# The transposed stream is made again for each use, and its 16 KB per partition become a tenth weight tile

## The chip, the cores and the metric

One core of one Trainium2 chip. The metric is the device time of one execution in microseconds (us); the kernel before takes 1452.84 us (median of 3 runs, 1452.74 to 1452.98).

## The reference

One layer on 256 tokens of width 2048, all in fp32: a mixer (attention and a state-space scan behind shared projections), then `h = layer_norm(alpha * x + mix)`, and on that h

```
scores = sigmoid(h @ w_router);  two experts of 16 per token, from one group of four
moe    = sum_e combine[:, e] * ((silu(h @ w_gate[e]) * (h @ w_up[e])) @ w_down[e])
ple    = sigmoid(h @ w_ple_gate) * (p @ w_ple)          # w_ple_gate is 2048 x 2048
out    = layer_norm(alpha * h + moe + ple)
```

The weights of one expert are 24 MB and those of the per-layer gate (with `w_ple`) 18 MB, so some 400 MB are read for this second half.

## The kernel before, in words

`front` (to line 531) computes the mixer. `back` (from line 534) is the second half, and the change lies there.

**Weight tiles.** Every weight of the second half passes through tiles of 128x4096 fp32 (2 MB of 2^20 bytes, 16 KB per partition) that the class `Ring` (line 42) hands out. `plan_loads` (line 74) lists the loads in the order in which they are used: for each expert e four pairs of gate and up tiles ("g" and "u", 2 MB each) and four down tiles ("d"); behind an expert of `PLE_AT` the three parts of one chunk of the per-layer gate ("pg": 1, 2 and 1 MB, with 0.5 MB of `w_ple`). `take` gives a tile to the matmuls and puts its room behind the spare ones; `fill` issues the next loads into what is spare, on SP's queue, where each waits until the last matmul that read its room is done. The rooms go round, so with N of them a load waits for the use N tiles earlier. There are 2 tiles in `ring1`, 2 in `ring2`, 4 in `ring3` (line 540), and one that is used once (`bonus`, line 586): nine at the start, eight from expert 1 on. SP's queue issues loads and little else.

**The h and its transposed copy.** `h` (tokens on partitions, 16 KB per partition, normalised but without gain and bias) stays to the end. `hT` (line 567) is the same, transposed, with gain and bias: 16 blocks k of 128x256, made once in lines 593 to 606 by TensorE transposes of h into a PSUM tile with two blocks, whose even block VectorE and whose odd block ScalarE then writes to `hT`. Besides the router, three things read it: `ple_gate` (line 825), `residual` (line 906) and the body of `overflow` (line 847), which runs only if an expert got over 64 tokens. At the end `ln2` lies in its room (line 568): gain and bias of the last norm, written behind expert 13.

**The order of the work.** `phase()` (line 675) ties TensorE's instructions of a phase behind the last one of the phase before; inside a phase a scheduler orders them, at compile time. For each expert: `gate_up` (line 716; 128 matmuls of 128x64 by 512 columns, which run side by side in pairs), `hidden` (line 729) with the other half of the expert before (`return_half`, line 799), for experts 2, 4, 5 and 7 a chunk of `residual`, at expert 7 `overflow` with its branch, behind odd experts `gather` (line 694) of the tokens for the next two, then `down` (line 781), and behind experts 3, 7, 10 and 12 a chunk of `ple_gate`: for 16 blocks k and two halves t of the tokens a matmul of 128x128 by 512 columns, then 8 matmuls with `w_ple`. Behind `down` ScalarE and VectorE split its result (`split_y`, line 776).

**Small tiles.** The pool `mp` (line 538) has tags with one room each: "xg" and "y" (8 KB), "w2" (2 KB; `hid` and `sg` use it), "hidT" (2 KB). PSUM tags "mt" and "pl" have two banks each.

Of the kernel before, what the change touches and what calls it, by code (L numbers as in the profile page):

```python
# [7 lines left out]
F32 = mybir.dt.float32  # L8
# [17 lines left out]
R = 4  # L26
PLE_AT = (3, 7, 10, 12)
RES_AT = (2, 4, 5, 7)
# [13 lines left out]
class Ring:  # L42


    def __init__(self):
        self.loads, self.n, self.pools, self.spare, self.tiles = [], 0, [], [], {}
        self.once = None

# [18 lines left out]
    def take(self, key):  # L67
        t, j = self.tiles.pop(key)
        if j != self.once:
            self.spare.append(j)  # L70
        return t
# [462 lines left out]
def back(ctx, tc, i, out, fr, dbg=lambda *a: None):  # L534
# [4 lines left out]
    psum = ctx.enter_context(tc.tile_pool(name="psum2", bufs=1, space=PSUM))  # L539
    ring.add(ctx.enter_context(tc.tile_pool(name="ring3", bufs=1)), RING3)  # L540
    ring.fill()

# [23 lines left out]

    hT = mp.tile([128, KB, 256], F32, name="hT")
    ln2 = hT.rearrange("p (j k) t -> p j (k t)", j=2)
    stats(5)
# [23 lines left out]
    for k2 in range(8):  # L593
        ps = banks[k2].rearrange("p (k t) -> p k t", k=2)
        for r in range(2):
            k = 2 * k2 + r
            for t in range(NT):
                nc.tensor.transpose(ps[:, r, t * 128:(t + 1) * 128], h[:, t, k * 128:(k + 1) * 128], ident)
        for r in range(2):
            k = 2 * k2 + r  # L600
            if r:
                nc.scalar.activation(hT[:, k, :], ps[:, r, :], AF.Identity, bias=lnT[:, 1, k:k + 1],
                                     scale=lnT[:, 0, k:k + 1])
            else:
                nc.vector.tensor_scalar(hT[:, k, :], ps[:, r, :], lnT[:, 0, k:k + 1], lnT[:, 1, k:k + 1],
                                        op0=OP.mult, op1=OP.add)
# [5 lines left out]
    for k in range(KB):  # L612
        g = k % 4
        nc.tensor.matmul(pr4[32 * g:32 * g + 32], fr.wr[:, k, :], hT[:, k, :], start=k < 4, stop=k >= KB - 4)
    r4 = mp.tile([128, 256], F32, name="r4", tag="cm", bufs=2)
# [113 lines left out]
    def hidden(e, pgu, oh, between):  # L729
# [15 lines left out]
        for j in range(4):  # L745
            nc.tensor.transpose(ps[:, j, :], hid[:, j // 2 * 256 + j % 2:(j // 2 + 1) * 256:2], ident)  # L746
        hidT = mp.tile([128, 4, 128], F32, name="hidT")
        nc.scalar.activation(hidT, ps, AF.Copy)
# [56 lines left out]
    def down_last(e, hidT, cm):  # L805
        py = psum.tile([128, 2, 512], F32, name="py", tag="y", bufs=1)
        y = y_parts()
        for q in range(4):
# [11 lines left out]
            for t in range(NT):  # L820
                for dh in range(2):
                    c = 4 * dh + q
                    nc.vector.bn_stats(st[:, t, c, :], acc[:, t, c * 256:(c + 1) * 256])

    def ple_gate(c):
        cs = slice(c * 512, (c + 1) * 512)
        pg = [pl_psum() for _ in range(NT)]
        for g, (k0, k1) in enumerate(PLE_PARTS):
            w = v2(ring.take(("pg", c, g)), 512)
            for k in range(k0, k1):  # L830
                for t in range(NT):
                    nc.tensor.matmul(pg[t], hT[:, k, t * 128:(t + 1) * 128], w[:, k - k0, :],  # L832
                                     start=k == 0, stop=k == KB - 1)
            if k1 < KB:
                ring.fill()
# [11 lines left out]
    def overflow():  # L847
# [9 lines left out]
        with tc.If(n_over > 0):  # L857
            with tc.For_i(0, NE, 1) as e:
# [3 lines left out]
                hd = mp.tile([128, 512], F32, name="hd", tag="w2", bufs=1)  # L862
                ow2 = mp.tile([128, 2, 512], F32, name="ow", tag="y")
                ow = ow2[:, 0, :], ow2[:, 1, :]
                for fh in range(2):
                    pgs = [psum.tile([128, 512], F32, name="pgu", tag="gu", bufs=2) for _ in range(NT)]
                    pus = [pl_psum() for _ in range(NT)]
                    for k in range(KB):
                        for j, (src, pz) in enumerate(((i["w_gate"], pgs), (i["w_up"], pus))):
                            w = wload(ow[j], src, e, k // R * 128 * R + k % R, fh * 512, R)  # L870
                            for t in range(NT):
                                nc.tensor.matmul(pz[t], hT[:, k, t * 128:(t + 1) * 128], w,
                                                 start=k == 0, stop=k == KB - 1)
# [32 lines left out]
    def residual(c):  # L906

        for t in range(NT):
            ps = pl_psum()
            for r in range(R):  # L910
                nc.tensor.transpose(ps[:, r * 128:(r + 1) * 128], hT[:, R * c + r, t * 128:(t + 1) * 128], ident)
            a = acc[:, t, c * 512:(c + 1) * 512].rearrange("p (f r) -> p r f", r=R)
            nc.vector.scalar_tensor_tensor(a, ps.rearrange("p (r f) -> p r f", r=R), ALPHA, a, op0=OP.mult, op1=OP.add)

    last = None
    for e in range(NE):
        if e % 2 and e + 1 < NE:
            oh_next = onehot(e + 1)
        with phase():
            pgu = gate_up(e, xg)  # L920
# [3 lines left out]
        hidT, cm = hidden(e, pgu, oh, lambda c: last and return_half(*last, c))  # L924
        if e in RES_AT:
            with phase():
                residual(RES_AT.index(e))
        if e == OV_AT:
# [16 lines left out]
        if e == 0:  # L945
# [15 lines left out]
            nc.vector.tensor_copy(ovT, po)  # L961
            nc.gpsimd.dma_start(scro, ovT)
        if e in PLE_AT:
            with phase():
                ple_gate(PLE_AT.index(e))
        if e == LN2_AT:

            for j in range(2):
                for c in range(4):
# [47 lines left out]
```

## Time and profile before

| | us |
|---|---|
| median of 3 runs | 1452.84 |
| the profiled execution | 1453.28 |
| its span | 1451.2 |
| TensorE matmul busy in the span | 1358.4 (94%) |
| VectorE busy | 453.5 (31%) |
| ScalarE busy | 296.9 (20%) |
| GpSimd busy | 62.1 (4%) |
| moved by DMA, mean rate | 499.91 MB, 344 GB/s |
| mean granted TensorE clock | 0.984 |

The span is that of one execution; the 2.1 us between span and time of that execution lie outside of it. Matmuls are pipelined, so that the busy time of one overlaps the next: what TensorE takes for a stretch is read from start to start. A timeline row gives the start, the busy time, engine and line, and in brackets how long the engine had been idle before and what it waited for.

### The profile page before, as it was taken

The page shows a single profiled execution, that of the slowest core. Times are in us where ns is not written, and L with a number is a line of the kernel's source. Part 1 is how long each engine was busy: PE and PEld are TensorE (multiplying, and loading weights), DVE is VectorE, ACT ScalarE, POOL GpSimd, SP SyncE. Part 2 cuts the span into 40 slices and gives each one's busy share as a digit, 9 for nine tenths or more (in the row PEclk, how much of TensorE's full clock was granted, in tenths as well). Part 3 has the DMA queues.
Part 4 walks back from the last instruction along what each step waited for, and adds up shares of the span by engine and source line. Part 5 has one row for each costly group of instructions (what it writes and reads, how often), then busy time and mean ns, then how long its engine had stood idle before and what let it go on. Part 6 is the DMA issues. An engine that isn't in the chain of part 4 may idle for free. (4 is left out here: it accounts for less than half of the span.)

```text
span 1451.2 us, 15673 instructions
## 1 busy us (share of the span) xinstructions
PE 1358.4 (94%) x6595; PEld 735.2 (51%) x6595; DVE 453.5 (31%) x768; ACT 296.9 (20%) x477; POOL 62.1 (4%) x80
## 2 busy tenths in 40 slices
PE   7999999999988999889999886999989999999994
PEld 5877888787785343344334323433423343445332
DVE  4486784646553020220023112002211031020227
ACT  4475564545332010000001000100100010002000
POOL 3000011301000000000000000000000000000002
PEclk9999999999998999999999999999999999999997
DMA  8655446456937999999999999999999999999994
GB/s 276 200 166 184 160 147 201 147 188 226 357 126 321 427 426 427 427 427 413 428 425 427 427 427 420 359 406 426 427 427 413 427 428 421 419 425 426 427 393 159
DMA packets 89646, 499.91 MB, mean 344 GB/s; under 512 B 9684, under 2 KB 22396, under 8 KB 65252
## 3 DMA queue, kind: packets, MB, share of 16 engines
q1 hardware_dynamic: 88128, 495.41, 84.8%
q0 software_dynamic: 1408, 3.41, 0.8%
q8 instruction: 53, 0.87, 0.2%
q14 instruction: 21, 0.17, 0.0%
q10 hardware_dynamic: 36, 0.05, 0.0%
HBM read 496.68 MB, written 2.16 MB: 344 GB/s over the span
## 5 line engine op out<-in xcount | busy, mean ns | idle before, releaser
L724 PE MATMUL pgu<-ring,xg 128*64 128x512 f32 x2048 | 450.2, 595 | 33.1 <-DMA ring<-in_w_up 18.2
L724 PEld LDWEIGHTS pgu<-ring,xg 128*64 128x64 f32 x2048 | 145.7, 137 | 334.4 <-issue 289.1
L790 PE MATMUL py<-ring,hidT 128*64 128x512 f32 x960 | 210.8, 594 | 7.4 <-DMA ring<-in_w_down 6.4
L207 DVE TENSOR_TENSOR wl<-ring,wh 128x1024 fp32r<-128x1024 f32 x128 | 156.2, 1224 | 140.0 <-ACT wh L206 134.8
L206 ACT ACTIVATE wh<-ring 128x1024 fp32r<-128x1024 f32 x128 | 135.4, 1060 | 172.1 <-PE pj L213 144.7
L211 PE MATMUL pj<-wh,xh 128*128 128x512 f32 x384 | 153.8, 402 | 1.1 <-ACT xh L188 1.0
L212 PE MATMUL pj<-wl,xh 128*128 128x512 f32 x384 | 153.6, 400 | 0.0
L213 PE MATMUL pj<-wh,xl 128*128 128x512 f32 x384 | 152.6, 399 | 0.0
L790 PEld LDWEIGHTS py<-ring,hidT 128*64 128x64 f32 x960 | 67.0, 137 | 141.3 <-issue 124.4
L734 DVE TENSOR_TENSOR hid<-hid,pgu 128x512 f32<-128x512 f32 x16 | 11.0, 688 | 399.7 <-ACT hid L733 399.7
L832 PE MATMUL pl<-ring,hT 128*128 128x512 f32 x256 | 110.9, 594 | 0.0
L779 DVE TENSOR_TENSOR y<-py,y 128x512 fp32r<-128x512 f32 (+1 forms) x34 | 22.5, 660 | 223.8 <-ACT y L778 223.8
L733 ACT ACTIVATE hid<-pgu 128x512 f32<-128x512 f32 x16 | 9.6, 598 | 390.9 <-PE pgu L724 390.9
L768 DVE SCALAR_TENSOR_TENSOR acc<-bk,cw,acc 128x512 f32<-128x512 f32 (+1 forms) x128 | 81.7, 710 | 1.9 <-PE bk L763 1.9
L211 PEld LDWEIGHTS pj<-wh,xh 128*128 128x128 f32 x384 | 72.6, 189 | 18.3 <-ACT xh L188 2.1
L213 PEld LDWEIGHTS pj<-wh,xl 128*128 128x128 f32 x384 | 72.4, 189 | 16.6 <-DVE xl L189 0.2
L212 PEld LDWEIGHTS pj<-wl,xh 128*128 128x128 f32 x384 | 72.6, 189 | 16.1
L832 PEld LDWEIGHTS pl<-ring,hT 128*128 128x128 f32 x256 | 48.3, 190 | 62.6 <-issue 62.6
L703 PE MATMUL mt<-wr,h 128*128 128x128 f32 x512 | 64.0, 289 | 7.9 <-PEq L857 6.1
L778 ACT ACTIVATE y<-py 128x512 fp32r<-128x512 f32 (+1 forms) x34 | 19.5, 573 | 238.6 <-PE py L790 209.7
L703 PEld LDWEIGHTS mt<-wr,h 128*128 128x128 f32 x512 | 62.5, 204 | 10.3 <-PEq L857 6.3
L212 PE MATMUL pj<-wl,moh 128*128 128x512 f32 (+1 forms) x160 | 56.7, 354 | 0.5 <-DVE wl L207 0.5
(252 smaller groups left out, 934.8 us busy)
## 6 DMA issues: line engine op xcount, KB each, us to landing
ring<-in_w_gate SPq DMA_DIRECT2D x64, 2048.0 KB, 22.9
ring<-in_w_up SPq DMA_DIRECT2D x64, 2048.0 KB, 24.5
ring<-in_w_down SPq DMA_DIRECT2D x60, 2048.0 KB, 25.8
ring<-in_w_in SPq DMA_DIRECT2D x48, 1024.0 KB, 5.1
ring<-in_w_out SPq DMA_DIRECT2D x16, 1024.0 KB, 6.5
ring<-in_w_ple_gate SPq DMA_DIRECT2D x16, 1024.0 KB, 30.8
ring<-in_w_down SPq DMA_DIRECT2D x32, 256.0 KB, 6.0
xq<-in_x SPq DMA_DIRECT2D x8, 256.0 KB, 9.4
```

The lines of the kernel that those rows point to most:

```text
L206: nc.scalar.activation(h, v, AF.Copy)
L207: nc.vector.tensor_tensor(l, v, h.bitcast(F32), op=OP.subtract)
L211: nc.tensor.matmul(ps, ah, bh, start=first, stop=False)
L212: nc.tensor.matmul(ps, ah, bl, start=False, stop=False)
L213: nc.tensor.matmul(ps, al, bh, start=False, stop=last)
L703: nc.tensor.matmul(ps[:, k % 4], h[:, t, cols], oh[:, t], start=t == 0, stop=t == 1)
L724: nc.tensor.matmul(pgu[j][hs], xg[:, k, e % 2, :], w[:, r, fh * 512:(fh + 1) * 512], start=k == 0, stop=k == KB - 1)
L768: nc.vector.scalar_tensor_tensor(a, ps[dh], cw[:, t, e:e + 1], a, op0=OP.mult, op1=OP.add)
L778: nc.scalar.activation(yh, ps, AF.Copy)
L779: nc.vector.tensor_tensor(yl, ps, yh.bitcast(F32), op=OP.subtract)
L790: nc.tensor.matmul(py[hs, c, :], hidT[:, j, fh * 64:(fh + 1) * 64], w[:, r, dh * 1024 + c * 512:dh * 1024 + (c + 1) * 512], start=fb == 0, ...
L832: nc.tensor.matmul(pg[t], hT[:, k, t * 128:(t + 1) * 128], w[:, k - k0, :], start=k == 0, stop=k == KB - 1)
```

## The change

`hT` is no longer kept. For the router it is still made once, in two halves that lie in the rooms of "xg" and "y". Afterwards `turn` transposes two blocks of h at a time into an "mt" bank and writes them with gain and bias into a small tile `hb`, whose rooms are those of "w2" and "hidT" in turn; `ple_gate` calls it before each even k, `residual` twice per chunk. In `turn` the order is: two transposes of the even block, its write by VectorE, two transposes of the odd block, its write by ScalarE. The 16 KB become `ring4`, one tile more; from expert 13 on, that tile is not given out again and holds `ln2`. The second chunk of the gate comes behind expert 8 rather than 7, and its loads with it. `residual` moves from before `down` to behind it (so behind overflow and gather too), since "hidT" is in use until `down` is done. The `overflow` body makes its blocks anew as well.

```diff
-PLE_AT = (3, 7, 10, 12)
+PLE_AT = (3, 8, 10, 12)
...
-        self.once = None
+        self.once = self.retire = None
...
-        if j != self.once:
+        if j not in (self.once, self.retire):
             self.spare.append(j)
...
     ring.add(ctx.enter_context(tc.tile_pool(name="ring3", bufs=1)), RING3)
+    ring.add(ctx.enter_context(tc.tile_pool(name="ring4", bufs=1)), 1)
+    last_pool = len(ring.pools) - 1
     ring.fill()
...
-    hT = mp.tile([128, KB, 256], F32, name="hT")
-    ln2 = hT.rearrange("p (j k) t -> p j (k t)", j=2)
+    hT = []
+    for tag in ("xg", "y"):
+        part = mp.tile([128, 8, 256], F32, name="hT", tag=tag)
+        hT += [part[:, k, :] for k in range(8)]
...
+    def turn(dst, k2, n=2):
+        ps = mt_psum([128, n, 256])
+        for r in range(n):
+            k = n * k2 + r
+            for t in range(NT):
+                nc.tensor.transpose(ps[:, r, t * 128:(t + 1) * 128], h[:, t, k * 128:(k + 1) * 128], ident)
+            if r:
+                nc.scalar.activation(dst[:, r, :], ps[:, r, :], AF.Identity, bias=lnT[:, 1, k:k + 1],
+                                     scale=lnT[:, 0, k:k + 1])
+            else:
+                nc.vector.tensor_scalar(dst[:, r, :], ps[:, r, :], lnT[:, 0, k:k + 1], lnT[:, 1, k:k + 1],
+                                        op0=OP.mult, op1=OP.add)
+        return dst
+
+    def turned(k2):
+        return turn(mp.tile([128, 2, 256], F32, name="hb", tag=("w2", "hidT")[k2 % 2], bufs=1), k2)
...
             for k in range(k0, k1):
+                if k % 2 == 0:
+                    hb = turned(k // 2)
                 for t in range(NT):
-                    nc.tensor.matmul(pg[t], hT[:, k, t * 128:(t + 1) * 128], w[:, k - k0, :],
+                    nc.tensor.matmul(pg[t], hb[:, k % 2, t * 128:(t + 1) * 128], w[:, k - k0, :],
                                      start=k == 0, stop=k == KB - 1)
...
-        for t in range(NT):
-            ps = pl_psum()
-            for r in range(R):
-                nc.tensor.transpose(ps[:, r * 128:(r + 1) * 128], hT[:, R * c + r, t * 128:(t + 1) * 128], ident)
+        pss = [pl_psum() for _ in range(NT)]
+        for k2 in (2 * c, 2 * c + 1):
+            hb = turned(k2)
+            for t, ps in enumerate(pss):
+                for r in range(2):
+                    col = (2 * (k2 % 2) + r) * 128
+                    nc.tensor.transpose(ps[:, col:col + 128], hb[:, r, t * 128:(t + 1) * 128], ident)
+        for t, ps in enumerate(pss):
...
+        if e == LN2_AT:
+            ring.retire = last_pool
...
-        if e in RES_AT:
-            with phase():
-                residual(RES_AT.index(e))
         if e == OV_AT:
             overflow()
...
+        if e in RES_AT:
+            with phase():
+                residual(RES_AT.index(e))
         if e in PLE_AT:
...
+            ln2 = v2(ring.tile(last_pool), DM)
```

## Rows read from the trace of the kernel before

**Rows 1.** The page, its second part: the span in 40 slices of 36.3 us, busy share of the DMA engines in tenths and GB/s moved.
```profile
DMA  8655446456937999999999999999999999999994
GB/s 276 200 166 184 160 147 201 147 188 226 357 126 321 427 426 427 427 427 413 428 425 427 427 427 420 359 406 426 427 427 413 427 428 421 419 425 426 427 393 159
```

**Rows 2.** Timeline of TensorE in the gate and up matmuls of expert 3: the first and the last of eight tiles.
```profile
603.63 3.65 PE L724 MATMUL pgu<-ring,xg 128*64 128x512 f32 x16 [1.34 <-DMA ring<-in_w_gate]
...
637.87 3.65 PE L724 MATMUL pgu<-ring,xg 128*64 128x512 f32 x16 [1.26 <-DMA ring<-in_w_up]
```

**Rows 3.** Busy time in stretches of 10 us. Columns: stretch, its length, then busy us and instructions of TensorE (PE), weight load (PEld), VectorE (DVE), ScalarE (ACT) and GpSimd (POOL); granted TensorE clock, DMA share, GB/s.
```profile
450.00:460.00 10.00, 10.00 (x70) 8.76 (x70) 3.01 (x6) 3.02 (x8) 0.00 (x0) 0.85 0.45 190
460.00:470.00 10.00, 10.00 (x50) 3.41 (x48) 0.00 (x0) 0.00 (x0) 0.00 (x0) 1.00 0.70 269
...
920.00:930.00 10.00, 10.00 (x38) 3.70 (x35) 1.38 (x2) 1.20 (x2) 0.00 (x0) 1.00 0.60 220
...
950.00:960.00 10.00, 10.00 (x33) 3.82 (x33) 1.38 (x2) 1.20 (x2) 2.53 (x2) 1.00 0.88 342
```

**Rows 4.** Timeline of SP's queue before the first expert: the first of four tiles of `ring3`, then `bonus` and the three behind it.
```profile
428.22 0.34 SPq L83 DMA_DIRECT2D ring<-in_w_gate  x1
...
434.42 34.72 SPq L83 DMA_DIRECT2D ring<-in_w_down  x4
```

**Rows 5.** Timeline of TensorE from the last up tile of expert 7 to the first of expert 8.
```profile
886.93 3.65 PE L724 MATMUL pgu<-ring,xg 128*64 128x512 f32 x16 [1.26 <-DMA ring<-in_w_up]
...
901.21 10.13 PE L703 MATMUL mt<-wr,h 128*128 128x128 f32 x64 [6.10 <-PEq L857]
911.27 13.95 PE L790 MATMUL py<-ring,hidT 128*64 128x512 f32 x64
925.15 27.73 PE L832 MATMUL pl<-ring,hT 128*128 128x512 f32 x64
...
956.25 27.69 PE L724 MATMUL pgu<-ring,xg 128*64 128x512 f32 x128
```

**Rows 6.** The instructions of line 857 (the branch of `overflow`) on SP's queue: duration in ns, first and last start in us.
```profile
L857 SPq EVENT_SEMAPHORE  x8: 17/17/17, 916.6 to 924.8; - x8
```

**Rows 7.** Timeline of TensorE: the gate and up matmuls of experts 9 and 10 begin, the third chunk of the per-layer gate, expert 11 begins.
```profile
1001.20 27.64 PE L724 MATMUL pgu<-ring,xg 128*64 128x512 f32 x128
...
1053.40 13.90 PE L724 MATMUL pgu<-ring,xg 128*64 128x512 f32 x64
...
1106.37 27.73 PE L832 MATMUL pl<-ring,hT 128*128 128x512 f32 x64
...
1137.46 27.69 PE L724 MATMUL pgu<-ring,xg 128*64 128x512 f32 x128
```

**Rows 8.** Timeline of TensorE: expert 12 begins, its chunk of the gate begins, expert 15 begins, its `hidden` begins, the last matmuls.
```profile
1189.71 24.20 PE L724 MATMUL pgu<-ring,xg 128*64 128x512 f32 x112
...
1237.83 27.73 PE L832 MATMUL pl<-ring,hT 128*128 128x512 f32 x64
...
1376.99 20.77 PE L724 MATMUL pgu<-ring,xg 128*64 128x512 f32 x96
...
1407.05 1.20 PE L763 MATMUL bk<-y,cm 64*128 64x512 f32 x8
...
1430.32 0.96 PE L763 MATMUL bk<-y,cm 64*128 64x256 f32 x8 [0.47 <-ACT y L778]
```

**Rows 9.** Timeline of TensorE at expert 4: the eight transposes of a chunk of `residual` and what follows them.
```profile
728.48 1.09 PE L911 MATMUL pl<-ident,hT 128*128 128x128 f32 x8
729.51 2.80 PE L790 MATMUL py<-ring,hidT 128*64 128x512 f32 x12
```

**Rows 10.** Instructions of three lines: duration in ns (min/median/max), first and last start in us, form. The transposes of `residual`, and the two writes of `hT` out of PSUM.
```profile
L911 PE MATMUL pl<-ident,hT x32: 272/273/328, 586.1 to 894.8; 128*128 128x128 f32 x32
...
L605 DVE TENSOR_SCALAR hT<-bk,lnT x6: 535/542/544, 434.3 to 438.1; 128x256 f32<-128x256 f32 x6
...
L602 ACT ACTIVATE hT<-bk,lnT x6: 556/564/566, 434.9 to 438.7; 128x256 f32<-128x256 f32 x6
```

**Rows 11.** Timeline where `hT` is made. "py" is one PSUM tile of two banks that holds blocks 4 to 7; "bk" are other banks.
```profile
434.70 0.85 PE L598 MATMUL py<-ident,h 128*128 128x128 f32 x3
...
435.34 1.77 PE L598 MATMUL bk<-ident,h 128*128 128x128 f32 x12
435.59 0.55 DVE L605 TENSOR_SCALAR hT<-py,lnT 128x256 f32<-128x256 f32 x1
...
436.17 0.56 ACT L602 ACTIVATE hT<-py,lnT 128x256 f32<-128x256 f32 x1
...
436.94 0.60 PE L598 MATMUL py<-ident,h 128*128 128x128 f32 x4
```

**Rows 12.** Timeline in the router: a write out of PSUM and the matmul that waits for it.
```profile
440.37 0.39 ACT L616 ACTIVATE r<-mt 128x256 f32<-128x256 f32 x1 [1.11 <-PE mt L614]
440.81 0.40 PE L619 MATMUL mt<-sel,r 128*128 128x16 f32 x2 [0.47 <-ACT r L616]
```

**Rows 13.** Timeline of ScalarE and VectorE behind the `down` of expert 10, at the start of its chunk of the gate (the second split follows the same way).
```profile
1106.48 0.60 ACT L778 ACTIVATE y<-py 128x512 fp32r<-128x512 f32 x1 [16.35 <-PE py L790]
1107.11 0.69 DVE L779 TENSOR_TENSOR y<-py,y 128x512 fp32r<-128x512 f32 x1 [13.96 <-ACT y L778]
...
1108.47 0.69 DVE L779 TENSOR_TENSOR y<-py,y 128x512 fp32r<-128x512 f32 x1 [0.66 <-ACT y L778]
```

More of the change, by code (lines that the diff above doesn't have):

```diff
@@ L601, in back @@
             if r:
-                nc.scalar.activation(hT[:, k, :], ps[:, r, :], AF.Identity, bias=lnT[:, 1, k:k + 1],
+                nc.scalar.activation(hT[k], ps[:, r, :], AF.Identity, bias=lnT[:, 1, k:k + 1],
                                      scale=lnT[:, 0, k:k + 1])
             else:
-                nc.vector.tensor_scalar(hT[:, k, :], ps[:, r, :], lnT[:, 0, k:k + 1], lnT[:, 1, k:k + 1],
+                nc.vector.tensor_scalar(hT[k], ps[:, r, :], lnT[:, 0, k:k + 1], lnT[:, 1, k:k + 1],
                                         op0=OP.mult, op1=OP.add)
@@ L613, in back @@
         g = k % 4
-        nc.tensor.matmul(pr4[32 * g:32 * g + 32], fr.wr[:, k, :], hT[:, k, :], start=k < 4, stop=k >= KB - 4)
+        nc.tensor.matmul(pr4[32 * g:32 * g + 32], fr.wr[:, k, :], hT[k], start=k < 4, stop=k >= KB - 4)
     r4 = mp.tile([128, 256], F32, name="r4", tag="cm", bufs=2)
@@ L746, in hidden @@
             nc.tensor.transpose(ps[:, j, :], hid[:, j // 2 * 256 + j % 2:(j // 2 + 1) * 256:2], ident)
-        hidT = mp.tile([128, 4, 128], F32, name="hidT")
+        hidT = mp.tile([128, 4, 128], F32, name="hidT", tag="hidT", bufs=1)
         nc.scalar.activation(hidT, ps, AF.Copy)
@@ L862, in overflow @@
                 hd = mp.tile([128, 512], F32, name="hd", tag="w2", bufs=1)
-                ow2 = mp.tile([128, 2, 512], F32, name="ow", tag="y")
-                ow = ow2[:, 0, :], ow2[:, 1, :]
+                ow3 = mp.tile([128, 3, 512], F32, name="ow", tag="y")
+                ow = ow3[:, 0, :], ow3[:, 1, :]
                 for fh in range(2):
@@ L868, in overflow @@
                     for k in range(KB):
+                        hb = turn(ow3[:, 2, None, :256], k, 1)
                         for j, (src, pz) in enumerate(((i["w_gate"], pgs), (i["w_up"], pus))):
@@ L871, in overflow @@
                             for t in range(NT):
-                                nc.tensor.matmul(pz[t], hT[:, k, t * 128:(t + 1) * 128], w,
+                                nc.tensor.matmul(pz[t], hb[:, 0, t * 128:(t + 1) * 128], w,
                                                  start=k == 0, stop=k == KB - 1)
@@ L966, in back @@
         if e == LN2_AT:
+            assert last_pool not in ring.spare and last_pool not in [j for _, j in ring.tiles.values()]
+            ln2 = v2(ring.tile(last_pool), DM)
             for j in range(2):
```

## The prediction

> **What bounds the kernel now.** I read the page's slices first. From slice 13 (about 470 us) to the end of the experts the DMA engines move 420 to 428 GB/s nearly without a break [rows 1]; the reader should see a second half that is bound by its 400 MB of weights, with few holes. Then I looked for where TensorE waits for a weight tile: in expert 3 it starts a tile every 4.89 us ((637.87 - 603.63) / 7), and each has only 3.65 us of work [rows 2]. From the size, 2.097 MB at 427 GB/s, a tile is 4.91 us; I use that. Third, the holes of the DMA: one before the first expert, of 0.55 and 0.30 of two stretches of 10 us, 8.5 us [rows 3]; two around expert 7, where 220 and 342 GB/s instead of 427 are 4.8 and 2.0 us [rows 3].
>
> The first hole is a full ring. Five loads are issued at 428 to 434 us [rows 4] and fill all nine rooms; the next must wait for the first matmuls. The hole at 920 us is another thing: at the branch of the overflow SP's queue waits eight times, up to 924.8 [rows 6], and issues nothing meanwhile; that looks like a wait for every load in flight. The one at 950 us is a full ring again, while TensorE works 31.1 us on a chunk of the gate (1137.46 - 1106.37) [rows 7], for which only 4.5 MB (11 us) are loaded.
>
> Behind the chunks the bound changes hands: TensorE is late there and has no waits. An expert of even number without chunk or `residual` takes it 1001.20 - 956.25 = 44.95 us when no load is late [rows 5, 7]. Expert 10 before its chunk took 52.97 us [rows 7], so 8.0 of waiting; expert 12 took 48.12 [rows 8], 3.2; the gate and up of expert 15 took 30.06 instead of 27.6 [rows 5, 8], 2.5. So from expert 8 on TensorE waits for loads for 13.7 us in all; the rest of that time, to its last matmul at 1430.32 + 0.96 = 1431.28 [rows 8], is its own work.
>
> **The gain of a tenth tile.** Six loads instead of five go out at 428 us; the hole of 8.5 us holds another 4.9. From there to the last up tile of expert 7 the DMA runs without holes and TensorE waits for it, so that tile comes at 882.0 rather than 886.93 [rows 5]: **-4.9 us**. The extra work of the change in experts 2 to 5 (below, some 6 us for a chunk and 2 for each piece of `residual`) is covered by TensorE's waits there, 1.25 us at nearly every tile [rows 2]; were they used up, it would come at full price.
>
> **Expert 7 and 8, new order.** Without a chunk behind expert 7, TensorE goes on from 882.0: before, it took 38.2 us to the chunk at 925.15 [rows 5], with 1.0 for the old `residual` (729.51 - 728.48) [rows 9]. The new `residual` transposes 8 blocks there and 8 back, 16 x 0.13 = 2.1 us and some waits; I take 2.7. That gives 882.0 + 38.2 - 1.0 + 2.7 = 921.9, and 44.95 for expert 8: 966.9 at its chunk. The DMA has 16 tiles to bring for this (4 down, 12 of expert 8): 882.0 + 78.6 = 960.6, plus the stop at the branch, which the change keeps; I take the 4.8 us of before for it: 965.4, then 3.6 of work on that tile: 969.0. The DMA is later by 2.1, so 969.0 counts; if SP's wait is shorter than before, 966.9 does.
>
> **The price: transposing again.** Let x be what a chunk takes more than 31.1 us. Its 32 transposes are 32 x 0.13 = 4.1 us, from the eight of `residual` that took 1.03 [rows 9]; the 64 matmuls of a chunk stay. On top come waits. A write of a 128x256 block takes 0.54 us on VectorE and 0.56 on ScalarE [rows 10]; a transpose ends 0.27 us after its start [rows 10], and a handover costs some 0.05 (the matmul starts 0.05 behind the write's end) [rows 12]. Where `hT` is made, ScalarE's write of the odd block starts only when VectorE's of the even block is done (436.17 behind 435.59 + 0.55), and the next four transposes into that tile start behind both, at 436.94, though twelve into other banks went before them [rows 11]. I take from this that accesses of different engines to one PSUM tile go one after another. In `turn` the odd block's transposes then wait for VectorE's write of the even block: that write ends at 0.13 + 0.27 + 0.05 + 0.54 = 0.99 and they start at 1.04 us. The first two transposes of the next pair (other bank) fill the time up to 0.52, as the same rows show that ready work is put ahead. Then 0.52 us are empty. Behind that the two pairs' matmuls (8 x 0.43 = 3.4) cover the other writes. So 4 waits of 0.52 per chunk: x = 4.1 + 2.1 = **6.2 us**.
>
> [...]
>
> Bounds for x: below, 4.1, if the order leaves no wait; above, 4.1 + 8 x 0.78 = 10.3, if each pair of blocks waits out its own write (1.04 - 0.26) with nothing put between. The split of the down result occupies VectorE until 2.8 us into the chunk (1108.47 + 0.69 - 1106.37) [rows 7, 13]; if the first write comes behind it, 2.4 us more per chunk. I take nothing for it, as VectorE is free in the first 0.7 us, when that write is ready at 0.45.
>
> **The sum.** Expert 9 starts at 969.0 + 31.1 + x = 1000.1 + x, against 1001.20 [rows 7]. From there to the last matmul it was 430.1 us, with 13.7 of waits; these go if loads are ahead. They are: the last down tile of expert 10 arrives 26.25 tiles (two experts and a chunk), 128.9 us and some 2 for the small rows of the chunk, behind 965.4, at 1096; TensorE, with x = 6.2, wants it at 1006.3 + 52.2 (an odd expert, with its gather of 7.3) + 44.95 - 3.6 = 1099.9. For expert 12 the gap grows. Two chunks more pay x. Last matmul: 1000.1 + x + 430.1 - 13.7 + 2x = 1416.5 + 3x = 1435.1, against 1431.28: **+3.8 us**. The tail behind it is not touched. The giving up of the tile at expert 13 costs nothing: TensorE is behind its loads by then; with loads late it would cost up to 4.9. The `hT` for the router lies in "xg" and "y", whose next users wait for the router anyway: nothing. The sum is made in the profiled execution (1453.28 for a span of 1451.2, 0.44 above the median); the difference added to the median gives 1456.6 us.
>
> So the trade is: 4.9 + 13.7 gained, less 1.7 for `residual` and 2.1 for the late tile, which leaves 14.8; 3x paid. It turns at x = 4.9.
>
> **Rivals.** (a) *No wait is left in the chunks.* The scheduler puts a transpose pair earlier, between the matmuls, so that x = 4.1: the last matmul is at 1428.8, -2.5, and 1450.3 us; if SP's stop at the branch is also shorter, so that 966.9 counts, 1448.2. For it: ready work is put ahead [rows 11]. Against: a chunk has only two banks of "mt", and the matmuls come before the next pair in the program. (b) *The waits stay in program order*: x = 10.3, +16.1, 1468.9 us; with the first write behind the split, x = 8.6, 1463.8. For it: nothing in [rows 11] says what the scheduler expects of a write. (c) *The tile does not do what it is meant to*: if the sixth load waits for a room that is still in use, the lead of 4.9 is lost and it is 1461.5 us. Against: the room is of the same region as `ring3`, whose loads went out together [rows 4].
>
> **How the numbers follow.** A measurement of this kernel tells about 0.2%, 2.9 us, from no change. My forecast has 0.42 (a little over half of it above 1455.7), (a) 0.34 (two thirds of it below 1449.9), (b) 0.17, (c) 0.07. Slower: 0.26 + 0.17 + 0.05 = 0.48; same: 0.16 + 0.10 + 0.02 = 0.28; faster: 0.24. The range takes in (a) in most of its width and of (b) the late first write: 1449 to 1464; the forecast's own is 1453 to 1459.
>
> **What would show it.** Right: gaps of about 0.5 us on TensorE before every second pair of transposes; chunks of 37 us; expert 7's last up tile at 882; no waits for weights from expert 9 on; full-ring holes of the DMA late in the kernel, where TensorE is now the bound; SP's eight waits at the branch as before. Wrong: chunks of 35 us or over 40; TensorE still waiting for weights in expert 10 or 12; the last up tile of expert 7 still at 887; a granted clock below 1.00 in the chunks.

## The result and the profile after

The changed kernel takes 1468.17 us (median of 4 runs, 1467.14 to 1469.19), the kernel before beside it 1452.91 us: a ratio of 1.0104 [1.0086, 1.0121], 15 us slower. The forecast was 1456.6 us with a range of 1449 to 1464: the sign was right, the size was not. The profiled execution took 1468.56 us, with a span of 1466.8 us.

The page's slices of the kernel after, busy share of the DMA engines in tenths and GB/s:

```profile
DMA  8655445456938999999999999899999999997994
GB/s 269 201 166 180 159 156 188 158 185 247 350 140 367 428 426 427 427 416 427 425 426 427 427 428 423 367 411 407 428 421 419 379 427 414 424 380 321 428 392 146
```

Set against [rows 1], the thirteenth number, the slice that ends where the steady 427 GB/s begin, is 367 instead of 321: 1.8 MB more, most of the 2.1 MB of a sixth early load. The first gate and up matmuls of expert 0, after and before:

```profile
459.89 27.69 PE L730 MATMUL pgu<-ring,xg 128*64 128x512 f32 x128
...
458.25 27.69 PE L724 MATMUL pgu<-ring,xg 128*64 128x512 f32 x128
```

In exchange for the early load the last quarter has holes (379, 380, 321) where there were none. They are full rings: TensorE doesn't wait for a single weight tile behind expert 7. Its waits from 940 to 1450 us:

```profile
PE mt L837 <- DVE hb L842: 5.5, 12, 0.5
PE bk L769 <- ACT y L784: 1.9, 4, 0.5
```

The columns are us in total, times, longest. Before, the same view from 985 us on has 4.2 + 3.7 + 3.3 = 11.2 us of waits for loads (13.7 us in the prediction, which counts from start to start). So the bound moved from the loads to TensorE, as forecast, and what is lost must be on TensorE. Its timeline from the last up tile of expert 7, against [rows 5]:

```profile
883.66 3.65 PE L730 MATMUL pgu<-ring,xg 128*64 128x512 f32 x16 [1.26 <-DMA ring<-in_w_up]
...
902.21 9.00 PE L709 MATMUL mt<-wr,h 128*128 128x128 f32 x64 [11.37 <-issue]
911.14 13.95 PE L796 MATMUL py<-ring,hidT 128*64 128x512 f32 x64
925.03 0.66 PE L837 MATMUL mt<-ident,h 128*128 128x128 f32 x4
926.11 0.44 PE L837 MATMUL mt<-ident,h 128*128 128x128 f32 x2 [0.42 <-DVE hb L842]
...
930.59 0.69 PE L941 MATMUL pl<-ident,hb 128*128 128x128 f32 x2 [3.82 <-ACT hb L839]
...
933.27 29.16 PE L730 MATMUL pgu<-ring,xg 128*64 128x512 f32 x128
```

Two gaps are new. The branch of the overflow, ahead of the gather, costs 11.37 us of idle time where it cost 6.10. And the last piece of `residual`, which stands behind it now, takes 933.27 - 925.03 = 8.24 us, not 2.7: TensorE waits 3.82 us for a write of ScalarE. What held ScalarE, and SyncE's branch with the waits at its end (beside [rows 6]):

```profile
929.48 0.60 ACT L784 ACTIVATE y<-py 128x512 fp32r<-128x512 f32 x1 [16.72 <-SPq L883]
929.97 0.56 ACT L839 ACTIVATE hb<-mt,lnT 128x256 f32<-128x256 f32 x1
```
```profile
L883 SPq EVENT_SEMAPHORE  x8: 17/17/17, 899.7 to 929.4; - x8
...
L883 SPq COMPARE_BRANCH  x1: 50/50/50, 889.5 to 889.5; - x1
```

ScalarE's write of the down result stands until 929.4, the moment in which SyncE's eight waits end, and the write that `residual` needs is queued behind it. In the kernel before, the same write began as soon as `down` was done:

```profile
L857 SPq COMPARE_BRANCH  x1: 50/50/50, 911.2 to 911.2; - x1
```
```profile
925.27 0.60 ACT L778 ACTIVATE y<-py 128x512 fp32r<-128x512 f32 x1 [12.38 <-PE py L790]
```

There SyncE came to its branch at 911.2 and its waits ended at 924.8; now the chunk's loads no longer stand ahead of the branch, SyncE comes there at 889.5, and waits for all that is on its way, some eight tiles ((929.4 - 889.5) / 4.91). Behind the pause TensorE's granted clock is 0.69 for 10 us (column PEclk, third from the right; other columns as in [rows 3]), and the gate and up matmuls of expert 8 take 29.1 us instead of 27.6:

```profile
920.00:930.00 10.00, 6.34 (x32) 2.27 (x28) 0.55 (x1) 0.52 (x2) 0.00 (x0) 0.97 0.60 251
930.00:940.00 10.00, 9.15 (x34) 3.46 (x36) 3.89 (x5) 1.69 (x4) 0.00 (x0) 0.69 0.97 380
```

The chunk itself is as forecast. The start of the first of its four groups of two pairs, and the start of what follows the chunk:

```profile
979.78 0.66 PE L837 MATMUL mt<-ident,h 128*128 128x128 f32 x4
980.86 0.44 PE L837 MATMUL mt<-ident,h 128*128 128x128 f32 x2 [0.42 <-DVE hb L842]
981.13 3.60 PE L858 MATMUL pl<-ring,hb 128*128 128x512 f32 x8
...
1017.05 1.51 PE L730 MATMUL pgu<-ring,xg 128*64 128x512 f32 x6
```

1017.05 - 979.78 = 37.27 us, 6.2 more than 31.1, with one wait of 0.42 to 0.49 us in each group, ahead of the transposes of an odd block. The end, against [rows 8] (the first row is the broadcast of `ln2`):

```profile
1338.41 10.60 PE L928 MATMUL pl<-pT,ident 16*128 16x128 f32 x64
1348.94 1.98 PE L730 MATMUL pgu<-ring,xg 128*64 128x512 f32 x4
...
1446.08 0.96 PE L769 MATMUL bk<-y,cm 64*128 64x256 f32 x8 [0.48 <-ACT y L784]
```

The last matmul ends at 1447.04, against 1431.28 before and 1435.1 forecast.

### The profile page after: what moved, and what is told of

The parts are those of the page before. It is cut to its first block, busy times and chain, and to the rows that moved or that the text cites. A ratio compares the mean times of both kernels' runs of the same rounds, so it can differ in the third digit from the quotient of the medians.

```text
span 1466.8 us, 16114 instructions
## 1 busy us (share of the span) xinstructions
PE 1381.7 (94%) x6755; PEld 753.6 (51%) x6755; DVE 473.0 (32%) x808; ACT 318.2 (22%) x517; POOL 62.1 (4%) x80
## 5 line engine op out<-in xcount | busy, mean ns | idle before, releaser
L858 PE MATMUL pl<-ring,hb 128*128 128x512 f32 x256 | 115.2, 592 | 0.0
L842 DVE TENSOR_SCALAR hb<-mt,lnT 128x256 f32<-128x256 f32 x40 | 20.6, 539 | 183.2 <-PE mt L837 183.2
L709 PE MATMUL mt<-wr,h 128*128 128x128 f32 x512 | 63.1, 287 | 12.2 <-issue 11.4
L858 PEld LDWEIGHTS pl<-ring,hb 128*128 128x128 f32 x256 | 46.1, 190 | 45.9 <-issue 44.9
```

The lines of the kernel that those rows point to most:

```text
L709: nc.tensor.matmul(ps[:, k % 4], h[:, t, cols], oh[:, t], start=t == 0, stop=t == 1)
L842: nc.vector.tensor_scalar(dst[:, r, :], ps[:, r, :], lnT[:, 0, k:k + 1], lnT[:, 1, k:k + 1], op0=OP.mult, op1=OP.add)
L858: nc.tensor.matmul(pg[t], hb[:, k % 2, t * 128:(t + 1) * 128], w[:, k - k0, :], start=k == 0, stop=k == KB - 1)
```

## The experiments

Three sets of four kernels; each set has its own runs of the kernel before, and the ratios are to these. A difference of 0.0010 between two ratios is 1.45 us.

**1. `shift`: the code moved, nothing else.** Only the body that doesn't run gets longer.

```diff
+                pad = mt_psum([128, 512])
+                for _ in range(24):
+                    nc.tensor.transpose(pad[:, :128], h[:, 0, :128], ident)
                 oT = mp.tile([128, 2, 4, 256], F32, name="oT", tag="xg")
```

> The kernel after with 24 more transposes in the overflow's body, which does not run: only the place of the code behind the branch is moved. [...] Rival B (the gap is due to what TensorE does there and not to where the code lies): the gap stays 11.4 us. [...]

Measured: 1467.23 us, ratio 1.0090 [1.0071, 1.0110]. TensorE's timeline:

```profile
895.24 9.84 PE L709 MATMUL mt<-wr,h 128*128 128x128 f32 x64 [5.90 <-PEq L883]
...
918.89 0.66 PE L837 MATMUL mt<-ident,h 128*128 128x128 f32 x4
...
929.06 0.69 PE L944 MATMUL pl<-ident,hb 128*128 128x128 f32 x2 [8.45 <-ACT hb L839]
...
931.75 29.04 PE L730 MATMUL pgu<-ring,xg 128*64 128x512 f32 x128
```

The branch costs 5.90 us again, with no instruction more or fewer on TensorE up to there. And the 5.5 us are lost at once: the wait for ScalarE grows from 3.82 to 8.45 us. The gate and up of expert 8 begin 1.5 us earlier, by as much as the last up tile of expert 7 came earlier in this run (882.15). So the place of the code sets the gap, against rival B, and SyncE's waits set the end of `residual`.

**2. `body_pool`: the branch without SyncE's DMAs.**

```diff
-            nc.sync.dma_start(ow, src[0, bass.ds(e, 1), row0:row0 + (127 * step + 1):step, col0:col0 + 512]
+            nc.gpsimd.dma_start(ow, src[0, bass.ds(e, 1), row0:row0 + (127 * step + 1):step, col0:col0 + 512]
...
-                nc.sync.dma_start(ovc, scro[bass.ds(e, 1)].rearrange("o t p -> p (o t)"))
+                nc.gpsimd.dma_start(ovc, scro[bass.ds(e, 1)].rearrange("o t p -> p (o t)"))
```

> The kernel after with the DMAs of the overflow's body (which does not run) issued by GpSimd instead of SyncE. Theory A (SyncE waits at the end of the branch for every load in flight because the body issues on its queues, and ScalarE's first write of the down result waits for the same loads, since the body writes that room): SyncE's eight waits go, the loads go on through the branch, ScalarE's wait of 16.7 us goes, `residual` behind expert 7 falls from 8.2 us to about 3, the clock stays up in expert 8: 6 to 8 us faster than after, 1460 to 1462 us. The 11.4 us of TensorE's branch stay. Rival B (the wait of ScalarE comes from its own late start behind the branch): no change beyond 1 us.

Measured: 1463.60 us, ratio 1.0068 [1.0045, 1.0092], 5.2 us better than after by the ratios. In the compiled program, ScalarE's write of the down result has changed in this alone, what it waits for:

```
after:      L784 ACTIVATE y<-py 128x512 [waits DMAHW6,DMAHW7,DVE,PE]
body_pool:  L784 ACTIVATE y<-py 128x512 [waits DMASW4,DMASW5,DVE,PE]
```

So it waited for two of the semaphores that SyncE's loads count on, since the body, which writes the same room by DMA, counts on them too. Now it starts at 924.88, right behind `down`:

```profile
900.61 10.33 PE L709 MATMUL mt<-wr,h 128*128 128x128 f32 x64 [11.42 <-issue]
...
924.76 0.66 PE L837 MATMUL mt<-ident,h 128*128 128x128 f32 x4
...
926.93 0.44 PE L941 MATMUL pl<-ident,hb 128*128 128x128 f32 x2 [0.44 <-ACT hb L839]
...
928.61 27.69 PE L730 MATMUL pgu<-ring,xg 128*64 128x512 f32 x128
```

`residual` takes 3.85 us instead of 8.24, the matmuls of expert 8 27.6 us again, and the granted clock from 930 to 940 us is 1.00. The branch stays at 11.4. Theory A holds in its mechanism; the gain is 1 us under its range of 6 to 8.

**3. `res6`: the last piece of `residual` behind expert 6.**

```diff
-RES_AT = (2, 4, 5, 7)
+RES_AT = (2, 4, 5, 6)
```

> The kernel after with the last piece of `residual` behind expert 6 instead of expert 7 (RES_AT = (2, 4, 5, 6)). Theory A (behind expert 7 the piece costs 8.2 us because ScalarE stands behind the loads in flight at the end of the branch, and the pause costs another 1.5 us of clock in the gate and up of expert 8): behind expert 6 TensorE waits for weights anyway, so the piece is free there, and the kernel is 8 to 10 us faster than after: 1458 to 1460 us; the step from the last down matmul of expert 7 to the gate and up of expert 8 falls from 8.2 us to under 1. Rival B (the piece costs its 16 transposes, some 2 to 3 us, wherever TensorE is late, and the rest is lost elsewhere): 2 to 3 us faster, 1465 to 1466 us.

Measured: 1458.26 us, ratio 1.0034 [1.0021, 1.0047], 10.2 us better than after. The number fits, but its parts do not: the branch fell to 5.7 us (16 transposes more ahead of it moved the code, which fits `shift`), and 5.4 us of waits for loads came in expert 8. Three rows of it:

```profile
895.78 10.13 PE L709 MATMUL mt<-wr,h 128*128 128x128 f32 x64 [5.70 <-PEq L883]
...
947.72 3.65 PE L730 MATMUL pgu<-ring,xg 128*64 128x512 f32 x16 [2.44 <-DMA ring<-in_w_up]
...
967.27 3.65 PE L796 MATMUL py<-ring,hidT 128*64 128x512 f32 x16 [1.34 <-DMA ring<-in_w_down]
```

The sum: 8.2 and 1.5 for `residual`, 5.7 for the branch, 5.4 back, and 0.8 from an earlier expert 7, which makes 10.8; the last matmul is 10.5 us earlier. Two errors of the expectation cancelled.

**4. `no_turn`: the price of the transposes.**

```diff
-                if k % 2 == 0:
-                    hb = turned(k // 2)
                 for t in range(NT):
-                    nc.tensor.matmul(pg[t], hb[:, k % 2, t * 128:(t + 1) * 128], w[:, k - k0, :],
+                    nc.tensor.matmul(pg[t], h[:, t, k * 128:(k + 1) * 128], w[:, k - k0, :],
```

> The kernel after with the gate's matmuls reading blocks of h directly: the transposes and their writes in the four chunks are left out (so the gate is computed from the wrong operand). Theory A (each of the last three chunks pays 6.2 us for 32 transposes and four waits, the first one nothing): 3 x 6.2 = 18.6 us faster, 1449 to 1451 us, chunks of 31.1 us; loads are then nearly late again at experts 10 and 12, which could give back up to 2 us. Rival B (the chunks cost more than their own length, through ScalarE and VectorE being late behind them): over 22 us faster, under 1446 us. Rival C (the loads bind as soon as the chunks are shorter): under 14 us faster, over 1454 us.

Measured: 1447.93 us, ratio 0.9956 [0.9942, 0.9969], 21.5 us better than after; in the profiled executions the last matmul is 20.0 us earlier. The chunk behind expert 8 begins at the same moment as in after (979.77: the branch is 5.36 us, and the wait for ScalarE behind it 8.34) and takes 31.1 us. Three times 6.2 is 18.6; the other 1.4 us lie in the broadcast of ln2 (9.3 us instead of 10.5) and behind it. The time lies between the ranges of A (1449 to 1451) and B (under 1446); the trace decides for A, but for these 1.4 us, as the three chunks account for 18.6 of the 20.0 us. C falls.

**5. `nine`: without the tenth tile.**

```diff
-    ring.add(ctx.enter_context(tc.tile_pool(name="ring4", bufs=1)), 1)
-    last_pool = len(ring.pools) - 1
...
-        if e == LN2_AT:
-            ring.retire = last_pool
...
-            assert last_pool not in ring.spare and last_pool not in [j for _, j in ring.tiles.values()]
-            ln2 = v2(ring.tile(last_pool), DM)
+            ln2 = v2(mp.tile([128, 4096], F32, name="ln2"), DM)
```

> The kernel after without the tenth weight tile (ln2_g and ln2_b keep a room of their own). Theory A (the lead of the tenth tile is lost again at the branch: SyncE's waits there end when the loads in flight have landed, and with nine rooms these are one fewer but one later): the last up tile of expert 7 comes 4.9 us later than in after, at 888.5, SyncE's waits end at 929 to 930 as in after, `residual` takes 3 us instead of 8.2, and the kernel's time is that of after within 2 us: 1466 to 1470 us. Rival B (the lead counts to the end, as the prediction had it): 4.9 us slower than after, 1473 us.

Measured: 1470.64 us, ratio 1.0118 [1.0100, 1.0137]; the intervals of this and of after overlap.

```profile
889.53 3.65 PE L728 MATMUL pgu<-ring,xg 128*64 128x512 f32 x16 [1.26 <-DMA ring<-in_w_up]
...
902.63 9.74 PE L707 MATMUL mt<-wr,h 128*128 128x128 f32 x64 [5.94 <-PEq L881]
...
931.55 0.69 PE L939 MATMUL pl<-ident,hb 128*128 128x128 f32 x2 [3.63 <-ACT hb L837]
...
934.24 29.69 PE L728 MATMUL pgu<-ring,xg 128*64 128x512 f32 x128
```

The tile's lead is there at expert 7 (889.53 against 883.66, 5.9 us) and is 1.0 us at the beginning of expert 8. SyncE's waits end at 930.4 here and at 929.4 in after, as theory A had it, but `residual` takes 8.05 us and not the 3 that it expected: the branch costs 5.9 us here, so TensorE comes to `residual` only 1.2 us later than in after and stands 3.6 us for ScalarE all the same. So most of the lead is hidden by the short branch, which is an accident of place. An estimate without it: 5.4 us later, behind SyncE's waits, with the 3.85 us of `body_pool` for `residual`, expert 8 would begin at 935.5, 2.2 us later than in after, and get 1.5 us of that back by its clock.

**6. `ple7`: the second chunk behind expert 7 again.**

```diff
-PLE_AT = (3, 8, 10, 12)
+PLE_AT = (3, 7, 10, 12)
```

> The kernel after with the second chunk of the gate behind expert 7, as before the change (PLE_AT = (3, 7, 10, 12)). Theory A (from expert 7 on TensorE's own work sets the end, so where the chunk stands counts for nothing): the time of after within 2 us, 1466 to 1470 us; the chunk costs 37 us there too; TensorE then waits for weights for 0 to 4 us in expert 10. Rival B (the move by one expert was worth something because the loads stand during the branch): over 3 us slower than after, 1471 us or more. Rival C (behind expert 7 the chunk hides the wait for ScalarE): over 3 us faster, 1465 us or less.

Measured: 1468.80 us, ratio 1.0112 [1.0088, 1.0136]: no difference from after. But two things cancel. With the chunk's loads ahead of the branch again, SyncE comes to it late:

```profile
L883 SPq EVENT_SEMAPHORE  x8: 17/17/17, 924.1 to 924.6; - x8
...
L883 SPq COMPARE_BRANCH  x1: 50/50/50, 906.5 to 906.5; - x1
```

ScalarE's write starts at 924.32, held by TensorE alone, and `residual` takes 3.75 us instead of 8.24. So it is the chunk's move behind expert 8 that brought SyncE to the branch early (889.5 in after, 894.2 in `nine`), and with it ScalarE's wait, as rival C supposed. What this saves is lost elsewhere: the chunk takes 40.3 us instead of 37.3, with a wait of 2.0 us for VectorE in its first group, and TensorE waits 1.8 us for down tiles and 0.7 for up tiles behind expert 7.

**7. `bank`: each block of a pair in a PSUM bank of its own.**

```diff
-        ps = mt_psum([128, n, 256])
         for r in range(n):
             k = n * k2 + r
+            ps = psum.tile([128, 256], F32, name="mt", tag=("mt", "gu")[r], bufs=2)
```

> The kernel after with each block of a pair in a PSUM bank of its own (the odd block in one of the banks of `gu`). Theory A (the wait of some 0.42 us before every odd block comes from VectorE's write of the even block in the same bank): the four waits of a chunk go, the chunk takes 35.2 to 35.8 us instead of 37.3, `residual` behind expert 7 stays at about 8 (ScalarE stands), and the three chunks give 5 to 6 us: 1462 to 1463 us. Rival B (the order of the instructions, not the bank, makes the wait): the chunks stay at 37 us, 1468 us.

Measured: 1464.33 us, ratio 1.0076 [1.0059, 1.0092], 4 us better than after. The chunk behind expert 8:

```profile
976.86 1.09 PE L837 MATMUL mt<-ident,h 128*128 128x128 f32 x8
977.93 7.13 PE L858 MATMUL pl<-ring,hb 128*128 128x512 f32 x16
...
1012.52 5.80 PE L730 MATMUL pgu<-ring,xg 128*64 128x512 f32 x26
```

It takes 35.66 us, 1.6 less, and has no wait left: eight transposes at a time, 4.2 us for all 32. This kernel too has the short branch (5.49 us) and loses it to ScalarE (a wait of 8.59 us). Theory A holds, with 4 us instead of 5 to 6; the edit gives the transposes two banks more as well, and they now come in another order.

**8. `combo`: the edits of 2, 3 and 7 together.**

> The three mends together: the last piece of `residual` behind expert 6, the DMAs of the overflow's body on GpSimd, a bank for each block. Theory A (branch 11.4, `residual` with its clock 9.7, three chunks 2 us each, and no load late since SyncE does not stop): 5.5 + 9.7 + 6 = 21 us faster than after, 1446 to 1449 us, faster than before; the chunk behind expert 8 begins at 964 to 966. Rival B (the loads bind as soon as TensorE is that early): 1451 us or more, with TensorE's waits for weights in experts 8 to 12.

Measured: 1450.72 us (10 runs), ratio 0.9978 [0.9968, 0.9987]: faster than before.

```profile
896.02 10.02 PE L709 MATMUL mt<-wr,h 128*128 128x128 f32 x64 [5.77 <-PEq L883]
...
919.75 27.64 PE L730 MATMUL pgu<-ring,xg 128*64 128x512 f32 x128
...
966.66 1.09 PE L837 MATMUL mt<-ident,h 128*128 128x128 f32 x8
...
1428.22 0.96 PE L769 MATMUL bk<-y,cm 64*128 64x256 f32 x8 [0.48 <-ACT y L784]
```

The time is just above the range of A (1446 to 1449) and just below that of B (1451 or more). The last matmul is 17.9 us earlier than in after; the sum said 21. The chunk begins at 966.66, not at 964 to 966, with 1.5 us of waits for down tiles in expert 8; the chunks give 1.6 us each, not 2.

**9. `combo_nine`: `combo` with the edit of 5.**

> The three mends together, but without the tenth weight tile. Theory A (once nothing stands at the branch, the lead of the tenth tile reaches the end): the last up tile of expert 7 comes 4.9 us later than with ten tiles and so does the end: 4 to 6 us slower than the three mends with ten tiles, about the time of before (ratio 0.9995 to 1.003). Rival B (the tile gives nothing even so): a ratio of 0.9970 to 0.9990, as with ten tiles.

Measured: 1457.28 us (10 runs), ratio 1.0016 [1.0005, 1.0027]; the last up tile of expert 7 comes at 890.18 instead of 883.09, and the last matmul 7.2 us later than in `combo`. With nothing in its way at the branch the tile is worth its lead to the end: 5.5 us by the ratios. Theory A holds.

**10. `before_pool`: the kernel before with the edit of 2.**

> The kernel before with the DMAs of the overflow's body issued by GpSimd. Theory A (the loads' stop of 4.8 us at the branch goes, but the ring is then full that much earlier in the chunk behind expert 7, and the hole at 950 us grows by as much; in the kernel before nothing on TensorE's path waits for ScalarE there): the same time within 2 us, a ratio of 0.9985 to 1.000. Rival B (the 4.8 us reach the end, since TensorE waits for loads for 13.7 us behind it): a ratio of 0.9965 to 0.9972.

Measured: 1453.59 us (10 runs), ratio 0.9994 [0.9983, 1.0004]. Its stretches, against [rows 3]:

```profile
920.00:930.00 10.00, 10.00 (x40) 3.61 (x37) 1.38 (x2) 1.19 (x2) 0.00 (x0) 1.00 1.00 426
...
940.00:950.00 10.00, 10.00 (x25) 4.42 (x24) 0.00 (x0) 0.00 (x0) 0.00 (x0) 1.00 0.90 357
950.00:960.00 10.00, 10.00 (x31) 3.91 (x31) 1.37 (x2) 1.19 (x2) 2.23 (x2) 1.00 0.53 192
```

The hole at 920 us is gone, and at 940 to 960 there are now 1.6 + 5.5 = 7.1 us of it, where 4.8 and 2.0 were at two places. A hole behind which the ring fills up anyway was worth nothing here.

**11 and 12. `spread` and `before_spread`: chunks where TensorE waits for weights.** In after, with the edits of 2 and 7, and in before, with the edit of 2:

```diff
+PLE_AT = (2, 5, 8, 11)
+RES_AT = (1, 3, 4, 6)
```

> The kernel after with the overflow's DMAs on GpSimd, a bank for each block, and the chunks and pieces moved to the front, where TensorE waits for weights (PLE_AT = (2, 5, 8, 11), RES_AT = (1, 3, 4, 6)). Theory A (in the three mends' kernel TensorE is busy without a break from expert 9 on and the DMA has holes of some 15 us there; with a chunk every third expert the loads bind nearly throughout, and the end comes when they are done): 12 to 17 us faster than the three mends, 1434 to 1439 us. Rival B (the chunks make the ring full and the loads stop in each): less than 6 us faster than the three mends, 1445 us or more.

> The kernel before (h transposed once and kept, nine tiles) with the overflow's DMAs on GpSimd and the same places for chunks and pieces (PLE_AT = (2, 5, 8, 11), RES_AT = (1, 3, 4, 6)). Theory A (it is bound by its loads, and only their holes at 920 and 950 us, 6.8 us together, can go): 5 to 8 us faster than before, a ratio of 0.9945 to 0.9965, and slower than the same places with ten tiles. Rival B (without the transposes it is faster than the same places with ten tiles): a ratio under 0.988.

Measured: `spread` 1445.42 us, ratio 0.9931 [0.9914, 0.9949], the fastest of all; `before_spread` 1448.72 us, ratio 0.9961 [0.9945, 0.9976]. `before_spread` does what was expected, and is 3.3 us slower than `spread` (their intervals just touch, their runs don't). `spread` gains 5 to 7 us on `combo` instead of 12 to 17. That is about the number of rival B, but not its reason: the loads hardly stop. From slice 25 to 38 the DMA's holes, against 427 GB/s, add up to 10.9 us in `combo` and to 5.7 in `spread`, so there were 5 us to gain and not the 15 that I had put there. Nor do the loads bind nearly throughout, as theory A had it: from 900 us on TensorE waits for six tiles, the last four in expert 15:

```profile
1397.47 3.65 PE L730 MATMUL pgu<-ring,xg 128*64 128x512 f32 x16 [1.39 <-DMA ring<-in_w_up]
...
1423.91 0.96 PE L769 MATMUL bk<-y,cm 64*128 64x256 f32 x8 [0.48 <-ACT y L784]
```

My estimate also put the end right behind the last loads and forgot that from the last up tile on TensorE has 27.4 us of work of its own (1424.87 - 1397.47). `spread` also shows the branch's second gap by itself:

```profile
915.08 0.77 PE L709 MATMUL mt<-wr,h 128*128 128x128 f32 x2 [5.52 <-PEq L883]
...
920.86 9.59 PE L709 MATMUL mt<-wr,h 128*128 128x128 f32 x62 [5.02 <-issue]
```

The first stop is that of the branch, 5.52 us. Two matmuls run, and at that point of the code TensorE stands another 5.02 us, with no semaphore to wait for that the profile shows. Beside both the traces have DMA packets of the queue q8, of kind "instruction" (56 packets, 0.92 MB on the page of after), each of 16384 bytes. In `spread` one starts at 912.43 and TensorE goes on at 915.08; the next starts at 918.35 and TensorE goes on at 920.86. In after they start at 894.02 and 899.69, and TensorE goes on at 902.21. In `shift` they start at 892.46 and 898.22; TensorE goes on at 895.24 and is at work when the second one comes. In before they start at 898.15 and 904.34; TensorE goes on at 901.21 and is at work then too. So in these four kernels a stop ends 2.5 to 3.1 us behind the start of such a packet, and the second packet starts 5.7 to 6.2 us behind the first. What ties a stop to its packet no run shows.

## Why the prediction was right in sign and wrong in size

The forecast for the last matmul was 1435.1; it came at 1447.04, 11.9 us later. Step by step:

- **The lead of the tenth tile** (-4.9): right. The tile comes at 883.66 instead of 882.0, but the first gate and up matmul, which stands ahead of all of this, came 1.64 us later than in before (459.89 against 458.25). From there to the last up tile of expert 7 it is 423.77 us in after and 428.68 in before, 4.91 less, and 423.6 to 423.8 in all eight kernels with ten tiles and the chunk places of after or of before. The start itself lies between 457.4 and 460.1 in these eight, so **1.7 us** of the miss is scatter of the mixer. `nine` and `combo_nine` need 430.7 and 430.2 us: without the tile the new order costs 1.6 to 2.0 us up to there, and the tile is worth that on top of its 4.9.
- **Expert 7 and 8, new order: the branch.** I carried its 6.1 us over as part of 38.2. It cost 11.37: **5.3 us**. This is one half of the step that failed. The gap follows the place of the code (`shift`), and is 5.4 to 6.6 us in ten of the fourteen kernels, before among them, and 11.4 to 11.9 in after, `body_pool` and `ple7`; in `spread` it falls into two. `nine` and `bank` issue as many matmuls ahead of the branch as after and differ in a few semaphore waits only, and have the short gap, so a few instructions decide. What sets the second stop no run shows; the traces have the packets told under `spread` beside it. No row that I had of before shows the second one; what I could have done is to give the stop a bound above what it was, since the edit adds code on both sides of it.
- **Expert 7 and 8, new order: `residual`** (2.7): it took 8.24, and a pause in front of expert 8 cost another 1.5 us of clock: **7.1 us** together. This is the other half. I had moved `residual` behind `down` and counted its own instructions, but not the queue that it was moved into: ScalarE, whose next instruction was the write of the down result. That write waits for SyncE's loads, because the overflow's body writes its room. In before the same wait was in the program; it was over at 924.8 [rows 6], ahead of ScalarE's write at 925.27, and a chunk that begins without ScalarE followed [rows 5]. The chunk's move behind expert 8, for which I counted no such cost, is what took that away (`ple7`). I saw SyncE's eight waits [rows 6], priced them as a hole of the loads alone, and asked who was queued behind SyncE only. `body_pool` shows the cause and 4.4 + 1.5 of the 7.1 us; the rest of `residual` is its waits for VectorE and ScalarE, some 1.2 us more than the 2.7.
- **The late load** (2.1 us over TensorE's 966.9): with TensorE this late it didn't bind: -2.1. The gather behind the branch was 1.1 us faster.
- **The price** (x = 6.2): 37.27 - 31.1 = 6.2. Right in mechanism and size: the waits are TensorE's for VectorE's write out of the same bank (0.42 to 0.49 us each), none is left in `bank`, where each block has a bank of its own and the chunk takes 35.66 us, and `no_turn` shows that three chunks pay.
- **The waits for loads that vanish** (-13.7): right; none is left, and from the start of expert 9 to the last matmul it is 429.99 us, 1.2 more than forecast.
- **The rest**, 1.2 us: the broadcast of ln2 takes 10.5 us instead of 9.3. In `no_turn` it is 9.3 again, in `bank` 11.9. Why was not tried.

1.7 + 5.3 + 7.1 - 2.1 - 1.1 + 1.2 = 12.1, against 11.9 measured.

Of the rivals, (a) and (b) fall with x = 6.2 and (c) with the lead. None of them had the branch or ScalarE in it. That (b) gave 1468.9 us, close to the 1468.17 measured, is a coincidence: its x was 10.3. The trade that I drew up (14.8 gained, 3x paid) was right about the parts that the change meant to touch. `nine` adds a point that I had not seen: the tile's gain hardly reached the end in after. Of its 5.9 us 1.0 was left at expert 8. The short branch of `nine` hid most of the rest; without it, by the estimate there, the wait for the loads in flight would still have taken all but some 0.7 us.

## What to carry to other kernels

When a step is moved, list for each engine that it uses what is queued ahead of it there and which semaphores that waits for; a wait that was over in time at the old place can be paid in full at the new one. A branch that is never taken can still make a later user of its rooms wait for the queues that its body would use, as ScalarE's write did here (until 929.4 us in after, against 924.88 in `body_pool`), so give that body a queue and rooms that the hot path does not share. And extra work belongs where the engine that does it waits: the chunks at experts 2, 5, 8 and 11, with the pieces of `residual` at 1, 3, 4 and 6, made either kernel faster (`spread` against `combo`, `before_spread` against `before_pool`), at the price of two lines.

## What the runs showed of the hardware

- TensorE's stop at a branch that is not entered is 5.4 to 6.6 us here in ten kernels. In four others some 5 us more come at or right behind it (5.02 in `spread`; 11.4 to 11.9 in all in the rest). An edit in code that never runs took the second stop away (`shift`, 5.90 us).
- In before, after, `shift` and `spread` these stops end 2.5 to 3.1 us behind the start of a packet of 16384 bytes on queue q8, of kind "instruction".
- After TensorE stood for 3.8 us in `residual`, its granted clock was 0.69 in the stretch from 930 to 940 us, and the 128 matmuls behind it took 1.5 us more; with waits of 0.44 us at the same place (`body_pool`) it was 1.00, and they took 27.6 us.
